# First group's attention output in rounded passes: three passes over 256 queries in place of fp32 matmuls over 128

## The chip, the core and the metric

The kernel runs on one core of a Trainium2 chip. The metric is the device time of one execution in microseconds, from the runs' times; the profile is of one execution more. The core has TensorE (PE: matmuls, with its weight loads shown apart as PEld), VectorE (DVE), ScalarE (ACT), GpSimd (POOL) and SyncE (SP), which issues most DMAs. Matmuls read their operands from SBUF and write to PSUM, which has eight banks of 512 fp32 columns.

## The reference, cut to what matters

A trunk of two layers over 512 tokens of width 1024: dilated attention and a feed-forward part, then a pooling mixer and a feed-forward part. The attention has three groups of eight heads of width 128; the first group looks at the last 128 tokens with stride 1:

```python
ATTN_PAIRS = ((128, 1), (512, 4), (2048, 16))
...
s = jnp.einsum('bnqhd,bnkhd->bnhqk', qb, kb) * (D ** -0.5)
...
p = jnp.exp(s - m)
den = jnp.sum(p, axis=-1, keepdims=True)
o = jnp.einsum('bnhqk,bnkhd->bnqhd', p / den, vb)
...
wts = jax.nn.softmax(jnp.stack(lses, axis=0), axis=0)
o = jnp.sum(wts[..., None] * o, axis=0).reshape(B, S, ATTN_WIDTH)
```

In the first group a block of 128 queries sees its own block of 128 keys and the one before. With four blocks that makes seven pairs of a query block and a key block.

## The kernel before

The work is tiled by 128 partitions. All large products run in rounded form: a number is split into a rounded part (type fp32r) and the remainder, and a product is the sum of three passes, rounded x rounded, rounded x remainder and remainder x rounded. `split` (L105) makes both parts: ScalarE rounds (L106), VectorE subtracts (L107). Weights come by DMA into `raw` tiles, are split into `whi` and `wlo`, and the split runs some steps ahead of its use (`pump`). Most products are done in seven half-size products in place of eight (`seven`, L463, for queries, keys and the first group's values; `values12`, L605, for the other two groups' values; `chain`, L516, later). The calls `behind(i)` in them place other work after the i-th of the seven, by the table that `between` (L990) gives. What each engine then runs in which order is set when the program is built, by a scheduler that orders each engine's instructions by its own estimate of when they are ready; each engine runs its own list strictly in order.

For each head h, spread over the products of heads h to h + 2:

- `scores0` (L686): query x key blocks of the first group in fp32, the largest score of each row, the exponentials into `s0`. Its 7 blocks of 128 keys stand in the order (query block 1: key blocks 0, 1), (2: 1, 2), (3: 2, 3), (0: 0). `scores12` does groups two and three into `s12`.
- `lay` and `merge` (L748): the groups' softmax sums are brought together; from them come factors `co`. VectorE multiplies the blocks of `s0` by them (L773, the three pairs first and the single block 6 last), ScalarE the blocks of `s12` (L776). The small steps ahead of it on VectorE are L768 to L771.
- `turn0` (L778): TensorE transposes the seven blocks of `s0` in fp32 (L785) into two PSUM banks, four and three, in order; ScalarE copies both banks into `t0` (L786). `turn12` does the same for `s12` into `t12` (L796, L797).
- `turn_values` (L670), for two heads at a time: the first group's values come out of `seven` as dimension x token; TensorE transposes them (L676), ScalarE copies them into `v0` (L677).
- `output` (L800): for the first group seven fp32 matmuls of 128 columns (L810 for query block 0, L812 and L813 for the others), values as the stationary operand, turned weights as the moving one; then eight for the other two groups (L819). ScalarE copies the first bank to `o` (L815), VectorE adds the second (L822).

In the odd heads from 3 on, one call of `seven` has `merge` behind its third and `turn_values` behind its fifth product, and the next has `turn0` behind its first. In the even heads `output` stands behind a product of the first and of the last `seven`. The last two heads have their `turn0`, `turn12` and `output` after the loop, among the first products with the output weights (L310 to L313). PSUM banks are handed out in the order of `RING`, and a bank is free again when the last reader is done.

Of the kernel before, what the change touches and what calls it, by code (L numbers as in the profile page):

```python
# [8 lines left out]
F32 = mybir.dt.float32  # L9
F32R = mybir.dt.float32r  # L10
# [5 lines left out]
P = 128  # L16
# [11 lines left out]
NT = S // P  # L28
# [23 lines left out]
def trunk(ctx: ExitStack, tc: tile.TileContext, xT, norms, w_first, w_qk, w_qkp, w_v0, w_v0p, w_v12, w_out, w_outp, w_pair, w_down, w_down0, w_down1, w_down2, w_pin, w_pgrp,  # L52
          consts, ident_in, invcnt_in, outT):
    nc = tc.nc
# [21 lines left out]
    ident = cpool.tile([P, P], F32, name="ident")  # L76
# [6 lines left out]
    def ps(tag=None):  # L83

        if tag is None:
            if turn["ring"] is None:
                tag = "ps"
            else:
                tag = RING[turn["ring"] % len(RING)]
                turn["ring"] += 1  # L90
        return psum.tile([P, S], F32, tag=tag, name=tag, bufs=BANKS[tag])
# [13 lines left out]
    def split(hi, lo, v):  # L105
        nc.scalar.activation(hi, v, AF.Copy)  # L106
        nc.vector.tensor_tensor(lo, v, hi.bitcast(F32), op=OP.subtract)  # L107
# [245 lines left out]
    def product(layer):  # L353
        return Product(KC, stream(layer)).add(range(KC)).p
# [228 lines left out]
    def in_a_row(t):  # L583
        return t.rearrange("p (r i b) -> p b i r", b=NT, r=NT)


    with tc.tile_pool(name="opool", bufs=1) as opool:
        early = [opool.tile([P, 2, S], F32R, tag=f"o{k}", name="early") for k in range(K2)]
        with tc.tile_pool(name="apool", bufs=1) as apool:
# [3 lines left out]
            QKV = {}  # L593
            A = {}
# [74 lines left out]

            def turn_values(h):  # L670

                t = apool.tile([P, NT, 2 * P], F32, name="v0")
                for c in range(2):
                    p = ps()
                    for b in range(NT):
                        nc.tensor.transpose(blk(p, b), blk(VT[c], b), ident)  # L676
                    nc.scalar.copy(t[:, :, c * P:(c + 1) * P], p.rearrange("p (b d) -> p b d", b=NT))  # L677
                QKV[h // 2, 0, 2] = t

            def blk(t, b, n=1):  # L680
                return t[:, b * P:(b + n) * P]
# [96 lines left out]
            def turn0(h):  # L778

                s0 = A[h]["s0"]  # L780
                t0 = apool.tile([P, 7 * P], F32, name="t0")
                for lo, n in ((0, 4), (4, 3)):
                    p = ps("ps" if h == HEADS - 1 else None)
                    for a in range(n):
                        nc.tensor.transpose(blk(p, a), blk(s0, lo + a), ident)  # L785
                    nc.scalar.copy(blk(t0, lo, n), blk(p, 0, n))  # L786
                A[h]["t0"] = t0

            def turn12(h):

# [9 lines left out]
            def output(h, tags=(None, None)):  # L800
                t0, t12 = A[h]["t0"], A[h]["t12"]
                once = tags[0] is not None

                def v0(b):
                    return blk(QKV[h // 2, 0, 2][:, b, :], h % 2)

                po = ps(tags[0])
                for b in range(NT):
                    if b == 0:
                        nc.tensor.matmul(blk(po, 0), v0(0), blk(t0, 6), start=True, stop=not once)  # L810
                    else:
                        nc.tensor.matmul(blk(po, b), v0(b - 1), blk(t0, 2 * b - 2), start=not once, stop=False)  # L812
                        nc.tensor.matmul(blk(po, b), v0(b), blk(t0, 2 * b - 1), start=False, stop=not once or b == NT - 1)  # L813
                o0 = o[h]
                nc.scalar.copy(in_a_row(o0), po.rearrange("p (b i r) -> p b i r", b=NT, r=NT))  # L815
                po = ps(tags[1])
                for r in range(NT):
                    for g in (1, 2):
                        nc.tensor.matmul(blk(po, r), blk(QKV[h // 2, 12, 2][:, r, :], h % 2 * 2 + g - 1),  # L819
                                         t12[:, r, g - 1, :], start=g == 1 and not (once and r),  # L820
                                         stop=g == 2 and (not once or r == NT - 1))
                nc.vector.tensor_add(o0, o0, po)  # L822
# [167 lines left out]
            def between(h, g):  # L990

                if g == 0:
                    return {0: [later(lay, h - 1)] if h == 1 else [], 2: [later(merge, h - 1)],
                            4: [later(turn_values, h - 1)] if h > 1 else []} if h % 2 else {
                        0: [later(lay, h - 1)], 1: [later(output, h - 2)], 2: [later(merge, h - 1)]}
                if g == (2 if h == 1 else 1):
                    return {0: [later(turn0, h - 1)], 2: [later(turn12, h - 1)], 4: [later(scores0, h)]}
                return {} if h % 2 else {2: [later(output, h - 1)]}
# [11 lines left out]
            for c in range(2):  # L1010
                p = product(0)
# [4 lines left out]
            scores12(0)  # L1016
            first = Product(KC, stream(0)).add(range(3))
            turn_values(0)
            first.add(range(3, KC))
            for h in range(1, HEADS):  # L1020
# [11 lines left out]
                if h == 1:  # L1032
                    for k in range(K2):
                        t = opool.tile([P, 2, S], F32, tag=f"o{k}", name="o")
# [26 lines left out]
            for c in range(2):  # L1061
                held["ow", c], t = slot("ow", kind=1)
                parts.append(t.rearrange("p a c -> p (a c)"))
            apart.split(*parts)
            output(last - 1, ("seed", "sum"))
            turn0(last)
            turn12(last)
            halve(last - 1)
# [14 lines left out]
            lo, hi = slice(0, H2), slice(H2, S)  # L1083
# [37 lines left out]
    with tc.tile_pool(name="fpool", bufs=1) as fpool:  # L1121
# [316 lines left out]
        with tc.tile_pool(name="work1", bufs=1) as wk:  # L1438
# [51 lines left out]
            t = wk.tile([P, 2 * S], F32, name="t", bufs=1)  # L1490
# [89 lines left out]
```

## Time and profile before

| | |
|---|---|
| median of 3 runs | 1239.25 us (1238.34 to 1239.36) |
| the profiled execution | 1239.08 us, span 1237.3 us |
| granted TensorE clock | 0.997 |
| busy PE / PEld | 1227.2 us / 1175.3 us |
| busy DVE / ACT / POOL | 1039.1 us / 697.4 us / 163.6 us |
| first group's outputs (L810, L812, L813) | 8 heads, first at 115 us, last at 451 us |

A row of the timeline or of the page gives the start in us, the duration in us, the engine, the line of the kernel, the operation and "written <- read", with the sizes (partitions x elements) and types, and the number of instructions merged into it; in brackets stands how long the engine sat idle before it, and what ended that. Names stand without their numbers: `t` is t0 or t12, `s` s0 or s12, `v` v0 or v12. An fp32 matmul makes two records. A line of the stretches gives the busy time of PE, PEld, DVE, ACT and POOL between two times, with their instructions, then the granted clock, the share of DMA engines busy, and GB/s. A line of the waits gives the waiting engine and line, the engine and line that it waited for, the total in us, how often and the longest.

### The profile page before, as it was taken

The numbers are of one execution on the slowest core, as the hardware profiler recorded it, in microseconds if no ns is written. First come the engines' busy times: TensorE is split into PE (matmuls) and PEld (weight loads), VectorE is DVE, ScalarE is ACT, GpSimd is POOL, SyncE is SP. The second block draws the span as 40 slices with busy tenths as digits, with TensorE's granted clock in tenths as the row PEclk, the third lists the DMA queues.
The fourth block names the chain that finished last, engine by engine and source line by source line (L and its number), as shares of the span: only waits on it lengthen the run. The fifth ranks groups of instructions, "written<-read, shape, count | busy, mean of one in ns | idle before, by whom it ended". The sixth has DMA issues, their size and how long they took to land.

```text
span 1237.3 us, 23682 instructions
## 1 busy us (share of the span) xinstructions
PE 1227.2 (99%) x9258; PEld 1175.3 (95%) x9258; DVE 1039.1 (84%) x1752; ACT 697.4 (56%) x1206; POOL 163.6 (13%) x153
## 2 busy tenths in 40 slices
PE   9999999999999999999999999999999999999997
PEld 8899999999999999899999999988789999999997
DVE  7987788879778899899778878798899877888876
ACT  6554554545455566466466566563546646656652
POOL 2121111111111110110111111000310111111100
PEclk9999999999999999999999999999999999999998
DMA  8456565655656454557766777554164777578641
GB/s 302 111 129 180 134 163 147 172 133 150 178 134 165 128 180 162 120 137 188 184 177 152 201 190 166 141 179 138 42 150 105 185 183 185 145 198 211 149 103 68
DMA packets 78943, 193.85 MB, mean 157 GB/s; under 512 B 7776, under 2 KB 16624, under 8 KB 78832
## 3 DMA queue, kind: packets, MB, share of 16 engines
q1 hardware_dynamic: 52272, 143.31, 34.8%
q0 software_dynamic: 25696, 48.25, 24.2%
q8 instruction: 72, 1.18, 0.4%
q10 hardware_dynamic: 864, 0.79, 0.2%
q14 instruction: 39, 0.32, 0.1%
HBM read 190.22 MB, written 2.10 MB: 155 GB/s over the span
## 4 chain that ended last, share of the span: by engine, by line
PE 91%; issue 4%; DVE 3%; DMA 1%; POOL 1%; ACT 0%; POOLq 0%; SPq 0%; DVEq 0%
PE sum L453 10%; PE sum L454 10%; PE sum L455 10%; PE seed L453 7%; PE seed L454 6%; PE seed L455 6%; PE ps L454 4%; PE ps L453 4%; PE ps L455 4%; PE seed L311 2%; PE seed L313 2%; PE seed L310 2%; PE ps L310 2%; PE ps L311 2%; PE ps L313 2%
## 5 line engine op out<-in xcount | busy, mean ns | idle before, releaser
L107 DVE TENSOR_TENSOR wlo<-raw,whi 128x1024 fp32r<-128x1024 f32 (+2 forms) x319 | 371.2, 1166 | 97.9 <-ACT whi L106 93.9
L106 ACT ACTIVATE whi<-raw 128x1024 fp32r<-128x1024 f32 (+2 forms) x319 | 323.0, 1016 | 213.8 <-PE seed L454 72.5
L186 POOL DMA_DIRECT2D raw<-w_pair x35 | 42.3, 1208 | 346.4 <-DMA raw<-w_pair 86.2
L454 PE MATMUL sum<-tt,whi 128*128 128x256 f32 x280 | 79.2, 283 | 0.0
L455 PE MATMUL sum<-tt,wlo 128*128 128x256 f32 x280 | 78.5, 280 | 0.0
L453 PE MATMUL sum<-tt,whi 128*128 128x256 f32 x280 | 78.5, 280 | 0.0
L106 ACT ACTIVATE halfhi<-rawhalf 128x512 fp32r<-128x512 f32 (+1 forms) x92 | 56.5, 614 | 29.5 <-PE sum L454 22.9
L208 DVE TENSOR_TENSOR raw<-raw 128x512 f32<-128x512 f32 (+1 forms) x92 | 60.9, 662 | 0.4
L207 DVE TENSOR_TENSOR raw<-raw 128x512 f32<-128x512 f32 (+1 forms) x92 | 60.9, 662 | 0.3
L107 DVE TENSOR_TENSOR halflo<-rawhalf,halfhi 128x512 fp32r<-128x512 f32 (+1 forms) x92 | 60.8, 661 | 0.0
L186 POOL DMA_DIRECT2D raw<-w_down x24 | 28.9, 1205 | 229.1 <-DVE hid L1167 74.2
L542 ACT COPY seed<-sum 128x256 f32<-128x256 f32 x62 | 22.2, 359 | 62.6 <-PE sum L455 62.6
L453 PEld LDWEIGHTS sum<-tt,whi 128*128 128x128 f32 x280 | 53.0, 189 | 0.0
L454 PEld LDWEIGHTS sum<-tt,whi 128*128 128x128 f32 x280 | 52.9, 189 | 0.0
L455 PEld LDWEIGHTS sum<-tt,wlo 128*128 128x128 f32 x280 | 52.6, 188 | 0.0
L454 PE MATMUL seed<-hy,whi 128*128 128x256 f32 x160 | 45.1, 282 | 0.0
L454 PE MATMUL sum<-hz,whi 128*128 128x256 f32 x160 | 45.0, 281 | 0.0
L455 PE MATMUL sum<-hz,wlo 128*128 128x256 f32 x160 | 45.0, 281 | 0.0
L453 PE MATMUL sum<-hz,whi 128*128 128x256 f32 x160 | 45.0, 281 | 0.0
L453 PE MATMUL seed<-hy,whi 128*128 128x256 f32 x160 | 44.9, 280 | 0.0
L455 PE MATMUL seed<-hy,wlo 128*128 128x256 f32 x160 | 44.9, 280 | 0.0
L186 POOL DMA_DIRECT2D raw<-w_qkp x19 | 23.4, 1234 | 147.5 <-DMA raw<-w_qkp 64.4
(666 smaller groups left out, 4699.3 us busy)
## 6 DMA issues: line engine op xcount, KB each, us to landing
raw<-w_pair SPq DMA_DIRECT2D x79, 512.0 KB, 4.8
raw<-w_qkp SPq DMA_DIRECT2D x38, 512.0 KB, 3.7
raw<-w_pair POOLq DMA_DIRECT2D x35, 512.0 KB, 6.6
raw<-w_down SPq DMA_DIRECT2D x32, 384.0 KB, 3.4
raw<-w_qkp POOLq DMA_DIRECT2D x19, 512.0 KB, 6.8
raw<-w_v SPq DMA_DIRECT2D x18, 512.0 KB, 4.8
rawhalf<-w_pair SPq DMA_DIRECT2D x35, 256.0 KB, 4.0
raw<-w_down SPq DMA_DIRECT2D x16, 512.0 KB, 4.7
```

The lines of the kernel that those rows point to most:

```text
L106: nc.scalar.activation(hi, v, AF.Copy)
L107: nc.vector.tensor_tensor(lo, v, hi.bitcast(F32), op=OP.subtract)
L186: nc.gpsimd.dma_start(b.rearrange("p (a c) -> p a c", a=2), self.src[:, None, 3 * q:].to_broadcast([P, 2, q]), accum_op=OP.add)
L207: nc.vector.tensor_add(a[:, :q], a[:, :q], b[:, :q])
L208: nc.vector.tensor_add(a[:, q:2 * q], a[:, q:2 * q], a[:, :q])
L310: nc.tensor.matmul(self.p[:, cols], w[0][:, s], mh[:, cols], start=self.done == 0, stop=False)
L311: nc.tensor.matmul(self.p[:, cols], w[0][:, s], ml[:, cols], start=False, stop=False)
L313: self.tail = nc.tensor.matmul(self.p[:, cols], w[1][:, s], mh[:, cols], start=False, stop=self.done == self.n)
L453: nc.tensor.matmul(dst, w.t[0][:, c], th, start=k == 0 and not onto, stop=False, skip_group_check=onto)
L454: nc.tensor.matmul(dst, w.t[0][:, c], tl, start=False, stop=False, skip_group_check=onto)
L455: last = nc.tensor.matmul(dst, w.t[1][:, c], th, start=False, stop=k == n - 1, skip_group_check=onto)
L542: copy = nc.scalar.copy(e, c)
```

## The change

The first group's output is written as three rounded passes for each key block b from 0 to 2, over the two query blocks b and b + 1 that see it: 256 columns each, nine in all. Key block 3, which only query block 3 sees, stays one fp32 matmul of 128 columns. For this the turned weights `t0` and the turned values `v0` become pairs of a rounded part and a remainder, straight out of PSUM, and the last block of each (`tend`, `vend`) is copied as before. The blocks of `s0` are transposed in another order, 6, 0, 1, 2 and 3, 4, 5, so that the columns of one key block lie side by side.

```diff
             def turn_values(h):
 
-                t = apool.tile([P, NT, 2 * P], F32, name="v0")
+                t = apool.tile([P, 2, NT - 1, 2 * P], F32R, name="v0")
+                end = apool.tile([P, 2 * P], F32, name="vend")
                 for c in range(2):
                     p = ps()
                     for b in range(NT):
                         nc.tensor.transpose(blk(p, b), blk(VT[c], b), ident)
-                    nc.scalar.copy(t[:, :, c * P:(c + 1) * P], p.rearrange("p (b d) -> p b d", b=NT))
-                QKV[h // 2, 0, 2] = t
+                    cols = slice(c * P, (c + 1) * P)
+                    split(t[:, 0, :, cols], t[:, 1, :, cols], blk(p, 0, NT - 1).rearrange("p (b d) -> p b d", b=NT - 1))
+                    nc.scalar.copy(end[:, cols], blk(p, NT - 1))
+                QKV[h // 2, 0, 2] = t, end
...
                 s0 = A[h]["s0"]
-                t0 = apool.tile([P, 7 * P], F32, name="t0")
-                for lo, n in ((0, 4), (4, 3)):
+                t0 = apool.tile([P, 2, 6 * P], F32R, name="t0")
+                end = apool.tile([P, P], F32, name="tend")
+                for lo, which in ((0, (6, 0, 1, 2)), (4, (3, 4, 5))):
                     p = ps("ps" if h == HEADS - 1 else None)
-                    for a in range(n):
-                        nc.tensor.transpose(blk(p, a), blk(s0, lo + a), ident)
-                    nc.scalar.copy(blk(t0, lo, n), blk(p, 0, n))
-                A[h]["t0"] = t0
+                    for a, b in enumerate(which):
+                        nc.tensor.transpose(blk(p, a), blk(s0, b), ident)
+                    n = min(4, 6 - lo)
+                    split(blk(t0[:, 0], lo, n), blk(t0[:, 1], lo, n), blk(p, 0, n))
+                    if lo:
+                        nc.scalar.copy(end, blk(p, n))
+                A[h]["t0"] = t0, end
...
-                def v0(b):
-                    return blk(QKV[h // 2, 0, 2][:, b, :], h % 2)
-
+                (vs, vend), (ts, tend) = QKV[h // 2, 0, 2], t0
                 po = ps(tags[0])
-                for b in range(NT):
-                    if b == 0:
-                        nc.tensor.matmul(blk(po, 0), v0(0), blk(t0, 6), start=True, stop=not once)
-                    else:
-                        nc.tensor.matmul(blk(po, b), v0(b - 1), blk(t0, 2 * b - 2), start=not once, stop=False)
-                        nc.tensor.matmul(blk(po, b), v0(b), blk(t0, 2 * b - 1), start=False, stop=not once or b == NT - 1)
+                for b in range(NT - 1):
+                    for n, (v, t) in enumerate(((0, 0), (0, 1), (1, 0))):
+                        nc.tensor.matmul(blk(po, b, 2), blk(vs[:, v, b], h % 2), blk(ts[:, t], 2 * b, 2),
+                                         start=b == n == 0, stop=False, skip_group_check=True)
+                nc.tensor.matmul(blk(po, NT - 1), blk(vend, h % 2), tend, start=False, stop=True, skip_group_check=True)
                 o0 = o[h]
                 nc.scalar.copy(in_a_row(o0), po.rearrange("p (b i r) -> p b i r", b=NT, r=NT))
```

In the rows of the changed kernel, lines behind the edits have other numbers: L773 reads L776 there, L776 reads L779, L785 reads L789, L819 reads L823, and the steps L769, L770 and L771 read L772, L773 and L774.

On TensorE, the output of head 0 in head 2's first product (`t_847` and `t_852` are t0, `v_663` is v0). Before, its list begins:

```order
L453 MATMUL sum<-h,whi 128x256
L454 MATMUL sum<-h,whi 128x256
L455 MATMUL sum<-h,wlo 128x256
L810 MATMUL sum<-t_847,v_663 128x128
L812 MATMUL sum<-t_847,v_663 128x128
L813 MATMUL sum<-t_847,v_663 128x128
```

and goes on with L812 and L813 twice more. Now it is:

```order
L453 MATMUL sum<-h,whi 128x256
L454 MATMUL sum<-h,whi 128x256
L455 MATMUL sum<-h,wlo 128x256
L815 MATMUL sum<-t_852,v_663 128x256 x9
L817 MATMUL sum<-tend,vend 128x128
L823 MATMUL ps<-t_896,v_997 128x128 x8
```

Seven matmuls of 128 columns have become nine of 256 and one of 128, at the same place between the same neighbours.

On VectorE, the merge of head 2, in head 3's first `seven` (`s_1546` and `s_1562` are s0, `qk_...` the new head's queries and keys). Before:

```order
L107 TENSOR_TENSOR wlo<-raw,whi 128x1024
L768 TENSOR_TENSOR dd<-ex,st 128x16
L495 TENSOR_TENSOR qk_1885<-seed,first 128x4x32x4
L769 TENSOR_TENSOR mx<-dd 128x8
L770 RECIPROCAL mx<-mx 128x8
L771 TENSOR_TENSOR co<-ex,mx 128x8
L773 TENSOR_SCALAR s_1546<-s_1546,co 128x256 x3
L773 TENSOR_SCALAR s_1546<-s_1546,co 128x128
L501 TENSOR_TENSOR sums<-seed,qk_1885 128x256 x2
L508 TENSOR_TENSOR qk_1886<-ps,sums 128x4x32x4
```

Now, from the same addition on:

```order
L772 TENSOR_TENSOR mx<-dd 128x8
L107 TENSOR_TENSOR v_2012<-ps,v_2012 128x3x128
L773 RECIPROCAL mx<-mx 128x8
L107 TENSOR_TENSOR v_2012<-seed,v_2012 128x3x128
L774 TENSOR_TENSOR co<-ex,mx 128x8
L501 TENSOR_TENSOR sums<-seed,qk_1904 128x256
L776 TENSOR_SCALAR s_1562<-s_1562,co 128x256 x3
L776 TENSOR_SCALAR s_1562<-s_1562,co 128x128
L501 TENSOR_TENSOR sums<-seed,qk_1904 128x256
L107 TENSOR_TENSOR wlo<-raw,whi 128x1024
L508 TENSOR_TENSOR qk_1905<-ps,sums 128x4x32x4
L509 TENSOR_TENSOR qk_1904<-sums,ps 128x2x32x4
```

The two remainders of the values stand between the small steps, one L501 addition has moved ahead of the four scalings, and a weight remainder ahead of L508; the two remainders of head 2's turned weights follow behind L509. The same three moves are in heads 5 and 7.

On ScalarE, the same place. Before:

```order
L767 ACTIVATE ex<-ex 128x16
L677 COPY v_1993<-ps 128x4x128
L677 COPY v_1993<-seed 128x4x128
L776 ACTIVATE s_1762<-s_1762,co 128x256 x4
L106 ACTIVATE whi<-raw 128x1024
L106 ACTIVATE halfhi<-rawhalf 128x512
L482 COPY first<-sum 128x256
```

Now:

```order
L770 ACTIVATE ex<-ex 128x16
L106 ACTIVATE v_2012<-ps 128x3x128
L106 ACTIVATE v_2012<-seed 128x3x128
L680 COPY vend<-ps 128x128
L106 ACTIVATE whi<-raw 128x1024
L779 ACTIVATE s_1781<-s_1781,co 128x256 x4
L680 COPY vend<-seed 128x128
L106 ACTIVATE halfhi<-rawhalf 128x512
L482 COPY first<-sum 128x256
```

The copies have become roundings of three blocks and copies of one, and a weight rounding has moved ahead of the scalings of `s12`. The first copy of `vend` waits for VectorE's remainder out of the same bank. In `turn0` the copy of `tend` waits in the same way, behind the next weight rounding.

After the loop, TensorE's list of the last head has six matmuls L310 to L313 between the transposes of `turn0` and those of `turn12`, where there were two. Farther on, in the output product and the first feed-forward part, weight remainders, activations and whole steps of a chain of matmuls change places with their neighbours on DVE, ACT and PE. The lists of SP and POOL are the same as before.

## Prediction

> **What bounds the kernel now.** I read the page first: engine totals, then the 40 slices, then the chain that ended last.
>
> ```profile
> PE 1227.2 (99%) x9258; PEld 1175.3 (95%) x9258; DVE 1039.1 (84%) x1752; ACT 697.4 (56%) x1206; POOL 163.6 (13%) x153
> PEclk9999999999999999999999999999999999999998
> PE 91%; issue 4%; DVE 3%; DMA 1%; POOL 1%; ACT 0%; POOLq 0%; SPq 0%; DVEq 0%
> ```
>
> TensorE is busy 99% of the span, its clock is granted throughout, and 91% of the last chain is matmuls. Since a busy matmul row can hide a stall, I then read the stretches, with the waits of the weight loads.
>
> ```profile
> 75.00:440.00 365.00, 365.00 (x3050) 362.78 (x3049) 297.28 (x472) 189.87 (x341) 58.01 (x61) 1.00 0.60 153
> 440.00:500.00 60.00, 60.00 (x429) 55.94 (x428) 51.96 (x93) 36.05 (x58) 4.28 (x6) 1.00 0.52 161
> ...
> PEld ps L402 <- POOL rcol L394: 2.2, 3, 1.2
> PEld sum L453 <- DVE x L1293: 1.3, 6, 0.3
> ...
> PEld ps L796 <- ACT t L786: 0.3, 1, 0.3
> ```
>
> From 75 to 440 us, where all but the last two of the changed outputs stand, weight loads fill 362.78 of 365 us. Not one of the waits listed lies in that stretch (the L796 one is the last head's, near 446 us). So TensorE bounds the stage: work taken from it shortens the span, and work given to VectorE (297.28 of 365 us busy) or ScalarE (189.87) costs only what it makes TensorE wait for.
>
> **The outputs on TensorE.** Head 3's, in the timeline of TensorE:
>
> ```profile
> 249.06 0.28 PE L454 MATMUL ps<-h,whi 128*128 128x256 f32 x1
> ...
> 251.65 0.28 PE L455 MATMUL seed<-tx,wlo 128*128 128x256 f32 x1
> 251.76 0.38 PE L810 MATMUL seed<-t,v 128*128 128x128 f32 x2
> ...
> 253.32 1.95 PE L819 MATMUL sum<-t,v 128*128 128x128 f32 x16
> ```
>
> The seven fp32 matmuls take 253.32 - 251.76 = 1.56 us, 0.222 each (each is two records). The 23 rounded passes of 256 columns from 249.06 to 251.65 make 22 steps in 2.59 us, 0.118 each; the new passes have their form. Nine of them and one fp32 matmul for the last block: 9 x 0.118 + 0.222 = 1.28 us, 0.28 less. Rounded and fp32 stretches alternate as often as before, so nothing is paid at the seams. Eight heads: **-2.2 us**, all on the bounding engine.
>
> By the Trainium skill, "TensorE: Matmul & The Clock Gate", section "Back-to-back issue gap", a warm pass of N columns takes N/2.4 + 2.5 ns, 109 ns for 256: an estimate of 1.20 us per head and -2.9 us in all. The rows here are slower than that rule, so I keep 0.118.
>
> **What VectorE and ScalarE get.** Per head, a remainder of 512 and one of 256 elements; per pair of heads, two of 384. Their nearest rows, from PSUM or of these sizes:
>
> ```profile
> 186.18 0.68 DVE L701 SCALAR_TENSOR_TENSOR s<-sum,b 128x512 f32<-128x512 f32 x1
> 186.78 0.55 DVE L707 SCALAR_TENSOR_TENSOR s<-ps,b 128x384 f32<-128x384 f32 x1
> ...
> 443.53 0.42 DVE L877 TENSOR_TENSOR diff<-o 128x256 f32<-128x256 f32 x1
> 443.86 0.42 DVE L894 TENSOR_TENSOR diff<-o 128x256 f32<-128x256 f32 x1
> ```
>
> From start to start 512 elements take 0.60 us and 256 take 0.33; on that line, 384 take 0.47. Together 8 x 0.93 + 8 x 0.47 = 11.2 us of VectorE, on the 67.7 us that it has free between 75 and 440. ScalarE's roundings replace copies of nearly the same size; new there are 16 copies of 128 elements, at most 0.36 us each (a 256-element copy, L482 below): under 6 us of 175 free. So the totals fit; only a place where TensorE soon needs VectorE's result can cost.
>
> I looked for these places with each wait's releaser. The tightest one that the change moves is in the odd heads from 3 on (three times), where the value remainders are put into the merge of the softmax groups. Before, head 3:
>
> ```profile
> 172.31 1.23 DVE L107 TENSOR_TENSOR wlo<-raw,whi 128x1024 fp32r<-128x1024 f32 x1 [0.56 <-PE seed L455]
> ...
> 174.49 0.16 DVE L769 TENSOR_TENSOR mx<-dd 128x8 f32<-128x8 f32 x1
> 174.70 0.20 DVE L770 RECIPROCAL mx<-mx 128x8 f32<-128x8 f32 x1
> 174.94 0.17 DVE L771 TENSOR_TENSOR co<-ex,mx 128x8 f32<-128x8 f32 x1
> 175.14 1.07 DVE L773 TENSOR_SCALAR s<-s,co 128x256 f32<-128x256 f32 x4
> 176.13 1.16 DVE L501 TENSOR_TENSOR sums<-seed,qk 128x256 f32<-128x256 f32 x2
> 177.21 1.11 DVE L508 TENSOR_TENSOR qk<-ps,sums 128x512 f32<-128x512 f32 x1
> ...
> 178.61 1.25 DVE L107 TENSOR_TENSOR wlo<-raw,whi 128x1024 fp32r<-128x1024 f32 x1
> ...
> 177.29 0.60 PE L785 MATMUL seed<-ident,s 128*128 128x128 f32 x4
> ```
>
> Two things tighten here. The first transpose at 177.29 used the block scaled first; now it is block 6, scaled last, done at 175.14 + 1.07 = 176.21: 1.08 us to spare. And the scalings come later: two remainders and one L501 addition now stand ahead of them. Remainders between the small steps also fill the latency after each, as these rows of the last head show:
>
> ```profile
> 434.11 0.15 DVE L769 TENSOR_TENSOR mx<-dd 128x8 f32<-128x8 f32 x1
> 434.18 0.68 DVE L207 TENSOR_TENSOR raw<-raw 128x512 f32<-128x512 f32 x1
> 434.78 0.19 DVE L770 RECIPROCAL mx<-mx 128x8 f32<-128x8 f32 x1
> 434.90 0.64 DVE L654 TENSOR_TENSOR v<-sum,sums 128x512 f32<-128x512 f32 x1
> 435.45 0.15 DVE L771 TENSOR_TENSOR co<-ex,mx 128x8 f32<-128x8 f32 x1
> ```
>
> With other work between, L769 and L770 hold the engine for 0.07 and 0.12, and L771 for about 0.08. From 174.49: 0.07 + 0.47 + 0.12 + 0.47 + 0.08 + 0.54 (half of 177.21 - 176.13) = 176.24; four scalings, 176.13 - 175.14 = 0.99, and 0.08 to the end of the last one's record: 177.31, against TensorE's 177.29. So the cover is used up to the last tenth. VectorE waited 0.56 us for TensorE at 172.31, so this lead is set anew each time and does not pile up. **+0.1 us** at each of three places, 0.2 to 0.3 in all; no gain is possible in this term. If remainders from PSUM cost as L501 does (0.54 per 256, so 0.81) and no latency is filled, the scalings end 2 x 0.81 + 0.54 = 2.16 later, and TensorE waits 1.1 us, three times: +3.3.
>
> A second rule bears on this. From L701 to L707 the engine starts again after 0.60 us though the record is 0.68 long. The Trainium skill, "VectorE: DVE Perf Modes", section "The DRAIN you can't avoid", has the next operation start only when the pipeline is empty; taken to the full record, each remainder is 0.55, the scalings end 0.16 later, and the sum loses some 0.5 us more. The start-to-start rows speak against that reading.
>
> **The new wait.** ScalarE's copy of the last block reads the bank that VectorE's remainder reads, and waits for it. Queued behind it are a weight rounding and the four scalings of the other groups:
>
> ```profile
> 172.79 0.59 ACT L677 COPY v<-ps 128x512 f32<-128x512 f32 x1 [0.40 <-PE ps L676]
> 175.20 1.71 ACT L776 ACTIVATE s<-s,co 128x256 f32<-128x256 f32 x4 [1.34 <-DVE co L771]
> 176.82 1.04 ACT L106 ACTIVATE whi<-raw 128x1024 fp32r<-128x1024 f32 x1
> 178.28 0.35 ACT L482 COPY first<-sum 128x256 f32<-128x256 f32 x1
> ...
> 180.90 0.60 PE L796 MATMUL ps<-ident,s 128*128 128x128 f32 x4
> ```
>
> The first remainder ends near 175.1, the copy near 175.4; the rounding, now ahead of the scalings, takes 1.0, so they run from 176.4 to 178.1, and their reader on TensorE comes at 180.90: nothing lost. In turn0 the same wait holds ScalarE until the second remainder: 177.2 + 0.5 for the late addition, 1.2 for a weight remainder that now stands ahead of L508, 1.4 for L508 and L509 (177.21 to 178.61), 0.93 for the two, 181.3. Behind it stand the copies of turn12's banks (0.59 each), then weight roundings, whose readers do not wait in the list above. At the last head the scheduler puts six 512-column matmuls, not two, between turn0's and turn12's transposes, so that both remainders end first: nothing, and the 0.3 us wait at L796 may shrink. No DMA moves: SP and Pool keep their order.
>
> **The sum.** The profiled execution took 1239.08 us (span 1237.3 and 1.8 around it); the median of the runs shown is 1239.25, 0.17 higher. 1239.08 - 2.2 + 0.2 = 1237.1, or 1237.2 against the median: that is the forecast, 0.16% faster, inside the 0.2% (2.5 us) below which a measurement of this kernel can hardly be told from no change.
>
> **The rivals.**
> 1. *More than the passes.* The reordering also removes small waits: L796 (0.3), and half of the 1.3 at the chains' L453, which VectorE's lateness sets. No stall at the odd heads: 1239.25 - 2.2 - 0.9 = 1236.2. For it: chains are among what the scheduler rearranged. Against: those waits recur with the same cause. The skill's 109 ns per pass would end near the same time (1236.4), but 22 steps of 0.118 speak against it. Chance 0.18, 0.03 of it for that rule.
> 2. *Given back.* Later stages wait for something that does not move, so TensorE's 2.2 us turn into waits after 500 us: 1239.3. Against it: weight loads wait there for other engines' answers to TensorE's own results, not for DMA, and DMA engines are 60% busy. Chance 0.1.
> 3. *Slower: the three merges.* The remainders are as dear as in the upper bound above: +3.3 - 2.2, 1240.4. It decides once a stall passes 0.75 us (2.2 / 3). The stretch fits to a tenth by my rows, so half a microsecond of error already costs 1.5. Chance 0.08.
> 4. *The passes are not single.* If rounded remainders of turned weights ran at fp32's 0.222 for each 128 columns, nine passes of 256 would take 9 x 0.444 = 4.0 us, each head 4.0 + 0.22 - 1.56 = 2.66 more than before: 1239.25 + 8 x 2.66 = 1260.5. Every rounded row of this form speaks against it. Chance 0.02.
>
> The forecast keeps 0.62. Its own range is 1236.8 to 1238.0: the odd-head term between 0 and 1 us. The whole range, 1236.0 to 1239.6, takes in rivals 1 and 2. Faster by over 0.2% (under 1236.8): rival 1 and a little of the forecast, 0.21. Slower by over 0.2% (over 1241.7): rival 4 and the far end of rival 3, 0.05. Same: 0.74.
>
> **What would show it.** Right: the pass line at 0.118 from start to start and an output stretch of 1.28 us up to L823; matmul starts at 177 us (shifted) with a gap of no more than 0.2 ahead of turn0's transposes; VectorE some 11 us busier before 440 us. Wrong: gaps of a microsecond ahead of those transposes (rival 3), longer waits after 500 us (rival 2), or passes spaced other than 0.118.

## The result and the profile after

The changed kernel takes 1237.16 us (median of 21 runs, 1236.14 to 1237.47), the kernel before in the same session 1238.67 (21 runs, 1238.17 to 1239.36). The ratio is 0.9986, with a 95% interval of 0.998 to 0.9992: faster by 1.5 us, inside the 0.2% named ahead as hard to tell from no change. The forecast was 1237.2 us, that is 2.0 less than the median that it started from (1239.25), and the time lies on it. That it does so to a tenth is luck: the change was 1.5 us, not 2.0, the kernel before ran 0.6 us faster this time than that median, and two terms of the sum were off in opposite directions, as follows.

The engines' totals on the page of the kernel after; under them, from the windows, the stretch with all but the last two of the changed outputs (busy time of matmuls, weight loads, VectorE, ScalarE and GpSimd, each with its count).

```profile
PE 1224.1 (99%) x9234; PEld 1171.1 (95%) x9234; DVE 1049.9 (85%) x1776; ACT 699.1 (57%) x1222; POOL 164.1 (13%) x153
...
75.00:440.00 365.00, 364.14 (x3035) 361.20 (x3034) 307.12 (x495) 192.39 (x357) 58.92 (x62) 1.00 0.60 154
```

VectorE has 10.8 us more work (1049.9 against 1039.1; 11.2 were worked out). New is the 364.14: between 75 and 440 us TensorE now stands still for 0.86 us where it had no gap at all. The waits view of the kernel after names the place (columns: total, times, longest):

```profile
PE seed L789 <- DVE s L776: 0.8, 2, 0.4
...
PEld sum L453 <- DVE x L1297: 1.3, 6, 0.3
```

L789 is the first transpose in `turn0` (L785 before), L776 the scaling that it waits for (L773 before). The 1.3 at the chains' L453 is what it was, so rival 1's second gain did not come. Its first, the 0.3 at L796, is off the list, but in TensorE's own starts it was worth only 0.05 us (446.14 - 445.86 = 0.28 before, 446.29 - 446.06 = 0.23 after).

The output of head 3 in the timeline of TensorE, then the three places at odd heads 3, 5 and 7: the last rounded pass ahead of the turn, and the turn's first four transposes.

```profile
251.28 1.22 PE L815 MATMUL seed<-t,v 128*128 128x256 f32 x9
...
252.55 1.95 PE L823 MATMUL sum<-t,v 128*128 128x128 f32 x16
...
176.73 0.28 PE L455 MATMUL sum<-h,wlo 128*128 128x256 f32 x1
177.12 0.63 PE L789 MATMUL seed<-ident,s 128*128 128x128 f32 x4
...
284.40 0.28 PE L455 MATMUL ps<-h,wlo 128*128 128x256 f32 x1
285.05 0.63 PE L789 MATMUL seed<-ident,s 128*128 128x128 f32 x4 [0.37 <-DVE s L776]
...
392.45 0.28 PE L455 MATMUL ps<-h,wlo 128*128 128x256 f32 x1
393.12 0.63 PE L789 MATMUL seed<-ident,s 128*128 128x128 f32 x4 [0.39 <-DVE s L776]
```

The output takes 252.55 - 251.28 = 1.27 us; 1.28 was forecast and 1.56 stood before. It is one of the slower ones: at heads 1, 3 and 5 the passes follow each other after 0.118 us and the output takes 1.27 or 1.28; at the other five heads they follow after 0.113 or 0.114, and it takes 1.24 (head 7: 451.29 - 450.05, a fence farther down). Before, each of the eight took 1.56. So the outputs came down from 12.48 to 10.02 us, by **2.46 us** (2.40 to 2.48 in four of the profiles that follow). Why some run at the shorter step is not known. Ahead of the turn, start follows start after 0.39, 0.65 and 0.67 us, where passes follow each other after 0.12: TensorE loses 0.27, 0.53 and 0.55, **1.35 us** in all. (The 0.37 and 0.39 in brackets are less, because the pass before counts as busy to its modelled end, and the first gap has no bracket at all; start to start shows the whole loss.)

VectorE at the same three places, after and, in the second fence, before (heads 5 and 7, with GpSimd's issues):

```profile
174.05 0.16 DVE L772 TENSOR_TENSOR mx<-dd 128x8 f32<-128x8 f32 x1
174.11 0.54 DVE L107 TENSOR_TENSOR v<-ps,v 128x384 fp32r<-128x384 f32 x1
174.57 0.18 DVE L773 RECIPROCAL mx<-mx 128x8 f32<-128x8 f32 x1
174.68 0.51 DVE L107 TENSOR_TENSOR v<-seed,v 128x384 fp32r<-128x384 f32 x1
175.10 0.16 DVE L774 TENSOR_TENSOR co<-ex,mx 128x8 f32<-128x8 f32 x1
175.17 0.62 DVE L501 TENSOR_TENSOR sums<-seed,qk 128x256 f32<-128x256 f32 x1
175.71 1.26 DVE L776 TENSOR_SCALAR s<-s,co 128x256 f32<-128x256 f32 x4
176.89 0.61 DVE L501 TENSOR_TENSOR sums<-seed,qk 128x256 f32<-128x256 f32 x1
...
283.47 1.44 DVE L776 TENSOR_SCALAR s<-s,co 128x256 f32<-128x256 f32 x4
284.82 0.60 DVE L501 TENSOR_TENSOR sums<-seed,qk 128x256 f32<-128x256 f32 x1
...
391.43 1.54 DVE L776 TENSOR_SCALAR s<-s,co 128x256 f32<-128x256 f32 x4
392.89 0.60 DVE L501 TENSOR_TENSOR sums<-seed,qk 128x256 f32<-128x256 f32 x1
```

```profile
283.27 1.07 DVE L773 TENSOR_SCALAR s<-s,co 128x256 f32<-128x256 f32 x4
284.05 1.25 POOL L186 DMA_DIRECT2D raw<-w_v  x1 [3.35 <-ACT s L776]
284.26 1.16 DVE L501 TENSOR_TENSOR sums<-seed,qk 128x256 f32<-128x256 f32 x2
...
391.41 1.24 DVE L773 TENSOR_SCALAR s<-s,co 128x256 f32<-128x256 f32 x4
391.81 1.25 POOL L186 DMA_DIRECT2D raw<-w_v  x1 [2.98 <-DMA raw<-w_v]
```

From the sum of the weights (L772) to the first scaling are 175.71 - 174.05 = 1.66 us; 1.75 was worked out. So the list of what stands ahead was right, and the remainders of 384 elements hold VectorE for 0.46 and 0.42, not more than forecast. But the four scalings take 1.18, 1.35 and 1.46 us to the next operation's start, against 0.99 before (284.26 - 283.27; the same at heads 3 and 7), and TensorE starts 0.14 to 0.15 after the last one's end (176.97 to 177.12; 284.91 to 285.05; 392.97 to 393.12), not at it.

What the scalings share with, in POOL's rows of the kernel after:

```profile
175.16 1.25 POOL L186 DMA_DIRECT2D raw<-w_v  x1 [3.04 <-ACT vend L680]
283.09 1.25 POOL L186 DMA_DIRECT2D raw<-w_v  x1 [3.21 <-ACT vend L680]
391.16 1.25 POOL L186 DMA_DIRECT2D raw<-w_v  x1 [3.32 <-ACT vend L680]
```

GpSimd issues the adding transfer of the next weights there, 1.25 us each time. Before, scalings and issue lay beside each other for 0.28, 0.2 and, at head 7, 0.59 us; now for 0.70, 0.87 and 0.98 us, and the longer the overlap, the slower the scalings (by 0.19, 0.36 and 0.47). From three rows that is a guess, to be tested. The kernel before has a hint of it: at head 7 the four scalings' record is 1.24 us long in place of 1.07, since the last of them, which began 0.4 us into the issue, took 0.45 us and not 0.28.

### The profile page after: what moved, and what is told of

Same layout as the page of the kernel before. It is cut to its first block, busy times and chain, and to the rows that moved or that the text cites. A ratio compares the mean times of both kernels' runs of the same rounds, so it can differ in the third digit from the quotient of the medians.

```text
span 1235.7 us, 23676 instructions
## 1 busy us (share of the span) xinstructions
PE 1224.1 (99%) x9234; PEld 1171.1 (95%) x9234; DVE 1049.9 (85%) x1776; ACT 699.1 (57%) x1222; POOL 164.1 (13%) x153
## 3 DMA queue, kind: packets, MB, share of 16 engines
q8 instruction: 72, 1.18, 0.4%
## 4 chain that ended last, share of the span: by engine, by line
PE 89%; issue 5%; DVE 4%; DMA 1%; ACT 0%; POOL 0%; SPq 0%; DVEq 0%; POOLq 0%; ACTq 0%
PE sum L453 10%; PE sum L454 10%; PE sum L455 10%; PE seed L453 6%; PE seed L454 6%; PE seed L455 6%; PE ps L454 4%; PE ps L453 4%; PE ps L455 4%; PE seed L311 2%; PE seed L313 2%; PE seed L310 2%; PE ps L310 2%; PE ps L313 2%; PE ps L311 2%
## 5 line engine op out<-in xcount | busy, mean ns | idle before, releaser
L186 POOL DMA_DIRECT2D raw<-w_pair x35 | 42.3, 1208 | 347.6 <-DVE halflo L107 58.9
L453 PE MATMUL sum<-tt,whi 128*128 128x256 f32 x280 | 78.5, 280 | 0.0
L186 POOL DMA_DIRECT2D raw<-w_down x24 | 28.9, 1205 | 227.8 <-DVE hid L1171 72.2
L453 PEld LDWEIGHTS sum<-tt,whi 128*128 128x128 f32 x280 | 53.1, 190 | 0.0
L453 PE MATMUL sum<-hz,whi 128*128 128x256 f32 x160 | 45.0, 281 | 0.0
L453 PE MATMUL seed<-hy,whi 128*128 128x256 f32 x160 | 44.9, 280 | 0.0
L186 POOL DMA_DIRECT2D raw<-w_qkp x19 | 23.4, 1234 | 150.9 <-DMA raw<-w_qkp 79.0
```

The source lines that it names most:

```text
L186: nc.gpsimd.dma_start(b.rearrange("p (a c) -> p a c", a=2), self.src[:, None, 3 * q:].to_broadcast([P, 2, q]), accum_op=OP.add)
L453: nc.tensor.matmul(dst, w.t[0][:, c], th, start=k == 0 and not onto, stop=False, skip_group_check=onto)
```

## The experiments

Theory: TensorE gains its 2.2 us or more in full, and 1.35 of it goes into waiting for the scaling of query tile 0, the last of four in VectorE's queue and the first that the turn needs. Three things make it late: the work queued ahead, GpSimd's issue beside it, and the 0.15 us from VectorE's end to TensorE's start. Rivals: the missing part was lost elsewhere (ScalarE's new waits, a later stage), or the passes gain less.

**1. Query tile 0 scaled first** (one line, and only VectorE's four scalings change places):

```diff
-                for b in (1, 2, 3, 0):
+                for b in (0, 1, 2, 3):
```

> As the changed kernel, but the merge scales the first group's block of query tile 0 first instead of last, so the block that the turn transposes first is ready first; no engine's order changes but VectorE's four scalings among themselves. Theory: the 1.35 us that TensorE waits ahead of the turn at heads 3, 5 and 7 (0.27, 0.53, 0.55) are waits for that last scaling, and go: 1237.16 - 1.35 = 1235.8 us, with the starts after head 7's output about 2.3 us ahead of the kernel before. Rival: the missing microsecond was lost elsewhere (start-up, ScalarE's new waits, a later stage): the waits go but the time stays at 1237.2, or they stay because something else is late behind them.

Measured: 1236.04 us against 1238.53 of before (ratio 0.9981, interval 0.9972 to 0.999). The transposes in it:

```profile
176.42 0.28 PE L455 MATMUL sum<-h,wlo 128*128 128x256 f32 x1
176.55 0.60 PE L789 MATMUL seed<-ident,s 128*128 128x128 f32 x4
...
283.83 0.28 PE L455 MATMUL ps<-h,wlo 128*128 128x256 f32 x1
283.95 0.60 PE L789 MATMUL seed<-ident,s 128*128 128x128 f32 x4
284.39 0.49 PE L789 MATMUL sum<-ident,s 128*128 128x128 f32 x3
284.94 0.38 PE L453 MATMUL seed<-h,whi 128*128 128x256 f32 x1
```

The transposes follow the last pass after 0.13 and 0.12 us: no wait, as expected, though the scalings beside GpSimd's issue stay slow in it too (1.31 and 1.47 us of record at heads 3 and 5). One wait of 0.30 us is new, at 284.94: start follows start after 0.55 there, against 0.25 in the kernel after. That pass waits for VectorE's semaphore, and VectorE's second L501 addition, queued behind the scalings, is done at 284.88; most likely the pass takes the bank that this addition reads. So what was next behind the removed wait was close.

**2. The old matmuls on the new operands.** All splits and the new order of transposes stay; the output goes back to seven fp32 matmuls, which read the rounded parts alone and leave the remainders out (`v0` and `w0` pick the blocks):

```diff
-                for b in range(NT - 1):
-                    for n, (v, t) in enumerate(((0, 0), (0, 1), (1, 0))):
-                        nc.tensor.matmul(blk(po, b, 2), blk(vs[:, v, b], h % 2), blk(ts[:, t], 2 * b, 2),
...
+                for b in range(NT):
+                    if b == 0:
+                        nc.tensor.matmul(blk(po, 0), v0(0), w0(0), start=True, stop=not once)
+                    else:
+                        nc.tensor.matmul(blk(po, b), v0(b - 1), w0(2 * b - 1), start=not once, stop=False)
+                        nc.tensor.matmul(blk(po, b), v0(b), w0(2 * b), start=False, stop=not once or b == NT - 1)
```

> As the changed kernel with all its roundings, remainders and its order of transposes, but the first group's output by seven fp32 matmuls again (it reads the rounded parts alone and leaves the remainders out of the sum). Theory: the change's cost without its gain; the waits of 0.3 to 0.55 us at heads 3, 5 and 7 stay and the time is the kernel before plus 1.35: 1238.67 + 1.35 = 1240.0 us. Rival (the gain is smaller than 2.2 us and the splits cost nothing): 1238.7 us, as before.

Measured: 1239.62 us against 1238.53 (ratio 1.0008, interval 0.9999 to 1.0017): 1.1 slower where 1.35 was expected; the interval just reaches no change, and the stage in the table below says the same, 1.26 slower. The waits ahead of the turn, by the same start-to-start reading, are 0.36, 0.43 and 0.55, together 1.34. The change without its passes costs this; with them it pays.

**3. A short issue on GpSimd.** The adding transfer covers one partition; every engine's order is that of the changed kernel:

```diff
-            nc.gpsimd.dma_start(b.rearrange("p (a c) -> p a c", a=2),
-                                self.src[:, None, 3 * q:].to_broadcast([P, 2, q]), accum_op=OP.add)
+            nc.gpsimd.dma_start(b.rearrange("p (a c) -> p a c", a=2)[:1],
+                                self.src[:1, None, 3 * q:].to_broadcast([1, 2, q]), accum_op=OP.add)
```

> As the changed kernel, but GpSimd's adding transfer of the weights covers one partition instead of 128 (so the sum of weight quarters is left out on the other 127); the order on every engine is the same. Theory: the three slow groups of four scalings (1.18, 1.35, 1.46 us from start to start against 0.99 before) are slow because GpSimd's issue of that transfer, 1.25 us, lies 0.70, 0.87 and 0.98 us of its length beside them; with a short issue they take 0.99 again, the waits become 0.08, 0.17 and 0.08 and the time 1237.16 - 1.0 = 1236.1 us. Rival (the scalings are slow for another reason, such as ScalarE's scalings of the other groups beside them): steps unchanged, 1237.2 us.

The trace at head 3, GpSimd and VectorE:

```profile
174.04 0.84 POOL L186 DMA_DIRECT2D raw<-w_v  x1 [1.98 <-DMA raw<-w_v]
175.66 1.06 DVE L776 TENSOR_SCALAR s<-s,co 128x256 f32<-128x256 f32 x4
176.64 0.60 DVE L501 TENSOR_TENSOR sums<-seed,qk 128x256 f32<-128x256 f32 x1
```

The issue is shorter (0.84) and, since the transfers ahead of it land sooner, over at 174.88, before the scalings start; these take 0.98 us to the next start here, and their records are 1.06, 1.07 and 1.06 at the three heads. The waits ahead of the turn are 0.15, 0.07 and 0.08 us (0.33 in all was expected). The time was not as expected: 1240.58 us against 1238.53 (ratio 1.0017, interval 1.0008 to 1.0026). That is not from this stage: at the last output TensorE is 2.2 us ahead of the kernel before (450.14 against 452.35, the table below), and at the end of the program still 2.1 (1226.48 against 1228.54). But its span of 1238.7 us goes on for 7.3 us after the last transfer of the result has been issued (at 1231.36), while that of the kernel after goes on for 3.2 (1232.49 to 1235.7). It is GpSimd that holds the end: every other engine is through by 1233.81, and GpSimd's closing drain runs from 1228.10 to 1237.88, in the kernel after from 1229.22 to 1232.40. Had it ended in time, the span would have been some 4.1 us shorter, about 1234.6: an estimate from these rows, and 1.1 under the kernel after, where 1.0 was expected. Why the drain is so long is not known, so this run speaks for the cause of the slow scalings and for the waits, not for a time. The rival falls too: ScalarE's scalings of the other groups run beside these as in the kernel after (175.76 to 177.45 at head 3), and nothing is slow.

**4. No remainders.** The roundings stay, VectorE's subtractions go, and all passes read the rounded parts (so the sum takes the rounded product three times; the values' split is changed in the same way):

```diff
-                    split(blk(t0[:, 0], lo, n), blk(t0[:, 1], lo, n), blk(p, 0, n))
+                    nc.scalar.activation(blk(t0[:, 0], lo, n), blk(p, 0, n), AF.Copy)
...
-                    for n, (v, t) in enumerate(((0, 0), (0, 1), (1, 0))):
+                    for n, (v, t) in enumerate(((0, 0), (0, 0), (0, 0))):
```

> As the changed kernel, but without VectorE's remainders: all nine passes read the rounded parts (the remainders are left out of the sum), order of transposes and of the scalings as in the changed kernel. Theory: VectorE has its old lead of about a microsecond, no wait at heads 3, 5 and 7, TensorE's gain alone: 1238.67 - 2.3 = 1236.4 us or a little less; the four scalings, earlier now, may still be slow where GpSimd's issue lies beside them. Rival (the new order of the transposes alone makes TensorE wait): waits of 0.3 to 0.5 us remain, 1237.2 us.

Measured: 1236.07 us against 1238.53 (ratio 0.998, interval 0.9971 to 0.9989), without a wait at the three places (transposes 0.12 us after the last pass at each). At head 5 the scalings had the longest record of all runs, 1.57 us, beside the issue, and it cost nothing, since they came a microsecond sooner:

```profile
282.46 1.57 DVE L776 TENSOR_SCALAR s<-s,co 128x256 f32<-128x256 f32 x4
282.74 1.25 POOL L186 DMA_DIRECT2D raw<-w_v  x1 [2.86 <-DMA raw<-w_v]
```

So neither the order of the transposes nor the slow scalings alone makes TensorE wait; it takes the work ahead of them, the remainders and the L501 addition, which here stays behind the scalings as before the change.

**5. The changed kernel and the version of experiment 1 again**, on one chip with the two that follow.

> The changed kernel itself, beside the next ones on the same chip. Every theory: about 1.5 us under the kernel before, with waits of about 0.3, 0.55 and 0.55 us ahead of the turn at heads 3, 5 and 7.

> The version with query tile 0 scaled first once more, on the same chip as the changed kernel: 1.4 us under the changed kernel and 2.4 to 2.5 under the kernel before, no wait at heads 3, 5 and 7.

Measured: 1237.66 us and 1236.47 us, before 1238.76: ratios 0.9991 (0.9982 to 1.0) and 0.9983 (0.9974 to 0.9991). The changed kernel waits 0.46, 0.44 and 0.32 us this time (1.22 in all): the three sizes change from one execution to another, their sum little. The version of experiment 1 has none this time.

**6. The last-scaled block transposed last in its bank:**

```diff
-                    for a, b in enumerate(which):
+                    for a, b in sorted(enumerate(which), key=lambda x: x[1]):
```

> As the changed kernel, scalings in its order, but in the first bank the turn transposes the block that is scaled last (block 6) as the last of four instead of the first; no engine's order changes otherwise. Theory: TensorE has three transposes, about 0.35 us, to do before it needs the last scaling: the waits shrink from 0.28, 0.54 and 0.55 to 0, 0.2 and 0.2, and the time is about 1.0 us under the changed kernel. Rival (what TensorE waits for is not that block's scaling but the whole tile, or VectorE's queue at large): the waits stay, and the time with them.

Measured: 1236.53 us against 1238.76 (ratio 0.9982, interval 0.9973 to 0.9991), 1.1 under the changed kernel. The waits have moved inside the group of four, which takes 0.60 us undisturbed:

```profile
177.22 0.73 PE L789 MATMUL seed<-ident,s 128*128 128x128 f32 x4
...
284.76 0.79 PE L789 MATMUL seed<-ident,s 128*128 128x128 f32 x4
...
392.56 0.60 PE L789 MATMUL seed<-ident,s 128*128 128x128 f32 x4
```

0.13, 0.19 and 0, with another 0.11 behind the second. It is this block's scaling that is waited for, not the tile as a whole.

**7. More work ahead of the scalings.** The values of odd heads are turned one product later; the scheduler then puts other work, and more of it, in the remainders' place:

```diff
-                            4: [later(turn_values, h - 1)] if h > 1 else []} if h % 2 else {
+                            5: [later(turn_values, h - 1)] if h > 1 else []} if h % 2 else {
```

> As the changed kernel, but the values of odd heads from 3 on are turned one product later, which puts their two remainders behind the scalings; in their place the scheduler puts the second L501 addition and a weight remainder of 1024 elements ahead of the scalings. Theory (what counts is all the work that VectorE has queued ahead of the last scaling): 0.07 + 0.54 + 0.12 + 0.54 + 0.08 + 1.14 = 2.5 us from the sum of the weights to the first scaling in place of 1.66, so each of the three waits grows by about 0.8 us less what a different share of GpSimd's issue changes: 2 us or more above the changed kernel, and slower than the kernel before. Rival (it is the value remainders themselves, or ScalarE's wait for them, that TensorE pays for): the waits go, 1.4 us under the changed kernel.

Measured: 1239.63 us against 1238.76 (ratio 1.0007, interval 0.9999 to 1.0016), 2.0 above the changed kernel on the same chip and 0.9 above the kernel before, where the interval just reaches no change. VectorE, GpSimd and TensorE at head 3:

```profile
175.31 1.25 POOL L186 DMA_DIRECT2D raw<-w_v  x1 [3.17 <-ACT v L106]
...
175.55 1.22 DVE L107 TENSOR_TENSOR wlo<-raw,whi 128x1024 fp32r<-128x1024 f32 x1
176.69 1.07 DVE L776 TENSOR_SCALAR s<-s,co 128x256 f32<-128x256 f32 x4
177.67 0.55 DVE L107 TENSOR_TENSOR v<-ps,v 128x384 fp32r<-128x384 f32 x1
...
176.66 0.28 PE L455 MATMUL sum<-h,wlo 128*128 128x256 f32 x1
177.90 0.63 PE L789 MATMUL seed<-ident,s 128*128 128x128 f32 x4 [0.96 <-DVE s L776]
```

No value remainder stands ahead of the scalings, and TensorE waits twice as long (1.12, 1.03 and 1.13 us): what counts is the whole queue. (At heads 5 and 7 the brackets name ScalarE, but there too the turn starts 0.15 us after the last scaling's end.) The scalings start after the issue has ended and take 0.98 us again, with the full transfer still under way (it lands 6.4 us after its issue began). At heads 5 and 7 it is the same, 0.98 us behind an issue that is over. So it is the issue on GpSimd that slows them, not the transfer.

**All runs side by side.** The stage is measured by TensorE's own starts: from the first transposes of the first turn (79.07 us before) to the start of the last head's second output product (452.35). All eight outputs lie between. The waits are those ahead of, in and just behind the turn at heads 3, 5 and 7.

| kernel | stage, us | against before | waits | without them |
|---|---|---|---|---|
| before | 373.28 | | 0 | |
| after | 372.02 | -1.26 | 1.35 | -2.61 |
| after, again | 372.00 | -1.28 | 1.22 | -2.50 |
| tile 0 first | 371.00 | -2.28 | 0.30 | -2.58 |
| tile 0 first, again | 370.69 | -2.59 | 0 | -2.59 |
| short issue | 370.92 | -2.36 | 0.30 | -2.66 |
| no remainders | 370.75 | -2.53 | 0 | -2.53 |
| block 6 last | 371.08 | -2.20 | 0.43 | -2.63 |
| more ahead | 373.84 | +0.56 | 3.28 | -2.72 |
| old matmuls | 374.54 | +1.26 | 1.34 | -0.08 |

The last column is the same for every kernel with the passes, 2.5 to 2.7 us, and nothing for the one without: the gain of the passes and the waits at three places make up the whole change. Ahead of the stage the kernel after is 0.20 us late (79.27 against 79.07), but over the ten profiles that start lies between 78.77 and 79.62, on either side. Behind this stage nothing more is lost: from that product to the last turn of the final norm's factors TensorE takes 776.19 us before and 776.31 after. These are the rows, before and then after:

```profile
452.35 1.95 PE L819 MATMUL seed<-t,v 128*128 128x128 f32 x16
1228.54 1.83 PE L402 MATMUL ps<-ident,rcol 128*128 128x128 f32 x8 [1.10 <-POOL rcol L394]
```

```profile
450.05 1.18 PE L815 MATMUL seed<-t,v 128*128 128x256 f32 x9
...
451.29 1.95 PE L823 MATMUL seed<-t,v 128*128 128x128 f32 x16
1227.60 1.16 PE L402 MATMUL ps<-ident,rcol 128*128 128x128 f32 x8 [1.10 <-POOL rcol L394]
```

The last group also shows why the spans differ by 1.6 us and these starts by 0.94: it took 1.83 us before and 1.16 after, and between 1.16 and 2.07 in the other profiles, the changed kernel's second one (2.03) among them. So it is scatter of the program's end and not shown to come from the change.

## Why the prediction was right, and where it was not

- **What bounds the kernel: right.** The waits and the windows put the whole change on TensorE's path, and VectorE's 10.8 us more show only where TensorE asks for a result.
- **-2.2 us from the outputs: right, somewhat small.** Measured over all eight heads they gave 2.46 us, since five of them run at 0.113 us per pass, not 0.118. The table gives 2.5 to 2.7; of the rest 0.05 is the wait at L796, and up to 0.2 is not traced to an instruction.
- **By the Trainium skill, "TensorE: Matmul & The Clock Gate", section "Back-to-back issue gap", 109 ns per pass:** the trace does not agree. Ahead of the turn, TensorE's passes start at 176.14, 176.26 and 176.38 us in the kernel after, 0.12 apart; the nine new ones and the fp32 matmul behind them take 1.24 to 1.28 us, where 1.20 followed from the rule. The section gives that rule for a pass by itself and says that in a stream of weight loads and passes both set the spacing; here each pass has its weight load.
- **"+0.1 us at each of three places": the step that failed.** It measured 0.27, 0.53 and 0.55, all over the 0.2 that the prediction named as the most it would allow. The place, its cause and the list of VectorE's work were right (1.66, 1.65 and 1.67 us to the first scaling for 1.75); wrong were two assumptions behind "four scalings, 176.13 - 175.14 = 0.99, and 0.08 to the end of the last one's record". One was that TensorE starts at that end: it takes another 0.14 to 0.15 us. The other, that an operation costs the same wherever it is moved: at head 3 the scalings began 1.14 us ahead of TensorE's turn (176.85 without a wait) in place of 2.15, came to lie beside GpSimd's issue and, over the three heads, took 1.18 to 1.46. Three times 0.15 and 0.19 + 0.36 + 0.47 make 1.47. Against that stand 0.27, since the scalings began that much sooner in all than worked out, and for it 0.06, the 177.31 - 177.29 of the forecast at three places. That is 1.26 of the 1.35; the 0.1 left is at head 5, where TensorE came to its turn 2.70 us after the sum of the weights (L772) began, in place of 2.81 before.
- **"No DMA moves: SP and Pool keep their order"** was right in order, but the order does not say what stands beside what. That is where the second assumption should have been caught: the rows of L186 at 284.05 and 391.81 were in the trace of before, the second one with a scaling that it made slower.
- **Rival 3, slower by the three merges**, was the right mechanism at a lower price: it decides from 0.75 us per place, and the places came to 0.45 on average. Experiment 7 shows it past that point, at 1.1: there the stage is 0.56 us longer than before.
- **ScalarE's new wait: right, it cost nothing here.** Its copy at head 3 waited for the remainder (below) and its second one ended at 177.65, with no reader of TensorE's late for it.

```profile
174.68 0.27 ACT L680 COPY vend<-ps 128x128 f32<-128x128 f32 x1 [1.41 <-DVE v L107]
...
177.40 0.25 ACT L680 COPY vend<-seed 128x128 f32<-128x128 f32 x1
```

- **The second rule, the pipeline that must be empty:** by "The DRAIN you can't avoid" (the Trainium skill, "VectorE: DVE Perf Modes") each remainder would hold VectorE for its record, 0.54 and 0.51; here the next operation started after 0.46 and 0.42 us. The trace sides with the start-to-start reading (the section itself adds that an operation that is not held starts sooner), and the loss had another cause.

The best version is the changed kernel with tile 0 scaled first: 1236.04 and 1236.47 us, 2.5 and 2.3 under the kernel before, and 1.2 under the changed kernel on the same chip.

## What to carry to other kernels

When an edit leaves a margin of a tenth of a microsecond by adding up durations, treat it as none: add the time from a producer's end to the consumer's start (0.15 us here), and look at what runs on the other engines in the stretch that the operation is moved to. Where a group of operations feeds a consumer that takes its parts in order, produce them in that order: here one line, with no work saved, was worth as much as the waits had cost. And read a loss from start to start: the idle time of the engine showed 0.86 of the 1.35 us.

## What the runs showed of the hardware

The issue of a transfer on GpSimd slows VectorE's scalings of fp32 elements, SBUF to SBUF. Four of them take 0.98 to 0.99 us alone. In the ten profiles every group that lay beside an issue of 1.25 us for 0.59 us or more was slower, with two shapes: where the issue began first, 1.11 to 1.46 us to the next start; where the scalings began first, only the last one or two were slower, as at head 7 before (above), where the next start was not late but the record was longer. One scaling of 256 elements took 0.35 us alone, most often 0.53 where it was hit, and at most 0.65. Not each one beside an issue was: at head 3 after, the first took 0.35 us though it began 0.55 us into the issue. So the length of the overlap does not set the loss: 0.82 us cost 0.12 in one profile, 0.87 cost 0.36 in another. Where only the end of the scalings lay beside the first 0.2 to 0.32 us of an issue, nothing was slower.

L501's additions, which read one operand from PSUM, show no such change: two take 1.08 us from start to start beside an issue at head 3 before (176.13 to 177.21, the issue from 175.85 to 177.10), that is 0.54 each, and one takes 0.53 away from it at head 5 after (284.82 to 285.35).

The Trainium skill, "SBUF — State Buffer", section "SBUF: two separate sides", has VectorE and GpSimd take a shared pair of ports by an exclusive lock, for VectorE's operations in a mode that uses two ports, with the loser blocked for the whole instruction, and its warning on transfers from GpSimd's queue tells of the transfer as the one that suffers. The trace agrees that the two collide, but here VectorE loses, and not for the whole issue: 0.12 to 0.47 us to the next start, at overlaps of 0.6 to 1.2 us. No run here shows which port it is.
